# First-stage operand tiles placed for TensorE, all seven kinds at one distance from the weights, and a second copy of one kind's high parts

## The chip, the cores and the metric

One core of a Trainium2 chip runs the whole program as one launch. The metric is device time in microseconds, from start to end of one execution; the number quoted is the median of three runs, and one more execution was profiled. "us" is microseconds, "ns" nanoseconds.

## The reference

One layer of a hybrid decoder, 512 positions of width 2048, all in float32. With `h = RMSNorm(x)` it computes

```
proj = h @ w_in                      # 2048 x 5648: q, k, v | z, xBC, dt
x    = x + concat(attention, ssd_scan) @ w_out
u    = causal_conv3(RMSNorm(x) @ w_up)          # 2048 x 11264
x    = x + (silu(u_gate) * u_val) @ w_down      # 5632 x 2048
```

The products with `w_in`, `w_out`, `w_up` and `w_down` are nearly all of the arithmetic. The rest (8 heads of attention, the chunked scan of 16 heads, norms, convolutions) runs beside them.

## The kernel before

**Split products.** Every float32 operand of a large product is held as two tiles of the one-pass type: `hi`, a rounded copy that ScalarE makes, and `lo`, the remainder that VectorE subtracts. A product is three matmuls that add up in PSUM: hi by hi, hi by lo, lo by hi. Each matmul is preceded by a load of its own 128x128 weights (PEld in the profile), and that load runs while the matmul before it streams its moving operand.

**First stages** (`w_in`, then `w_out`). The weights come in chunks of 128x1024, three `raw` buffers deep, and `issue_split` (line 243) makes of each piece of up to 528 columns an `hi` and an `lo` tile, three buffers of each, in the pool `w`. The activations lie in `A0..A15` (high parts) and `B0..B15` (low parts), 512 columns each, allocated right behind that pool. There are two ways to use a piece:
- `fm_uses` (line 639) and `wide_use` (line 657): the piece is the stationary operand, and A or B moves with 512 columns.
- `tok_use` (line 672): A or B is the stationary operand, and the piece moves, with 256 columns (v), 264 (z and dt of the first group) or 512 (z of the second group).

The order of the work between the pieces is fixed when the program is built, by the costs in `Paced` and by `advance`, which lets generators of the attention and the scan issue their parts between pieces.

**Second stage** (`w_up`, then `w_down`). A two-by-two scheme with seven products in the place of eight is used: each of 68 groups (44 of up, with 8 blocks of the contraction; then three passes of 8 groups of down, with 7, 8 and 7 blocks) makes seven products P1 to P7. The weights of a product are a sum or difference of raw blocks, split into `hi2` and `lo2` (three and two buffers of 128x1024, lines 1034 to 1051). The moving operand is one of seven kinds (`KT1`, `KT3`, `K11`, `KT2`, `K21`, `K22`, `KT4`), a tile [128, 2, 8, 256] with high parts at index 0 and low parts at index 1. P3 is the product whose kind is `K22`. The order of the products is a list, `items` (line 997): P5 of a group, P3 of the group before, P1, P4 of the group before, P6, P2, P7. Lines 1285 to 1292 issue a product: for each of the n blocks one matmul with the kind's high part (L1288) and one with its low part (L1289), both by the weights `hi2`; then n with the high part by `lo2` (L1291). So a product is 24 or 21 matmuls of 256 columns. `step_slot` (line 1256) then issues, in the same order on every engine's queue, events, the `lo2` split of the item two ahead, more events, and the `hi2` split three ahead.

The kinds of up are made once: five at the end of the first stages, `K22` and `KT4` by `x_split` (line 1126) at slots 2, 4, 5 and 6. Each pass of down makes its seven kinds anew from scratch memory, `b_load` and `b_split` (line 1088), two halves per kind, at slots written out by hand around the last groups of the pass before.

**Addresses.** Where a tile starts follows from the order and sizes of allocation. Take the *distance* of a matmul as the start of its moving operand less the start of the weights that are loaded beside it (those of the next matmul), modulo 512 bytes; a block of weights is 512 bytes wide, a moving block of 256 columns 1024, so the distance stays the same within a product. Before the change:
- Second stage: 448 bytes for six kinds, 0 for `K22`. `KT4` lies behind `K22` in the same pool with a spare tile of 112 floats (448 bytes) between them (line 1129).
- First stages: `hi` and `lo` are 528 floats, 2112 bytes, so each buffer is shifted by 64 bytes against the one before it, and the distance changes with the buffer and from one matmul of a triple to the next: for a stationary piece 384, 192, 384 in the first buffers, 320, 128, 320 in the second, 256, 64, 256 in the third; for a moving piece of 256 or 512 columns 128, 320, 128, then 192, 384, 192, then 256, 448, 256.

Of the kernel before, what the change touches and what calls it, by code (L numbers as in the profile page):

```python
# [20 lines left out]
F32 = mybir.dt.float32  # L21
F32R = mybir.dt.float32r
BF = mybir.dt.bfloat16
AF = mybir.ActivationFunctionType
OP = mybir.AluOpType
# [8 lines left out]
NF = FF // 128  # L34
# [15 lines left out]
PASSES = [(0, 7), (7, 8), (15, 7)]  # L50
# [10 lines left out]
KT1, KT3, K11, KT2, K21, K22, KT4 = range(7)  # L61
# [126 lines left out]
def body(ctx, tc, xT, wi, wz, wo, wu, wd0, wd1, wd2, pp, pf, outT, dbg={}):  # L188
    nc = tc.nc
    clk = {"pe": 0.0, "act": 0.0, "dve": 0.0, "pool": 0.0, "last": ("pe", 0.0)}  # L190
    V, A_, T, G = (Paced(e, k, clk) for e, k in
                   ((nc.vector, "dve"), (nc.scalar, "act"), (nc.tensor, "pe"), (nc.gpsimd, "pool")))

    consts = ctx.enter_context(tc.tile_pool(name="consts", bufs=1))
    pstack = ExitStack()
    psum = pstack.enter_context(tc.tile_pool(name="psum", bufs=4, space=bass.MemoryType.PSUM))
    dram = ctx.enter_context(tc.tile_pool(name="scratch", bufs=1, space=bass.MemoryType.DRAM))
    ab, cw, work = ExitStack(), ExitStack(), ExitStack()
    wpool = ab.enter_context(tc.tile_pool(name="w", bufs=3))
    abp = ab.enter_context(tc.tile_pool(name="ab", bufs=1))  # L200
    cpool = cw.enter_context(tc.tile_pool(name="c", bufs=1, side="right"))
    wk = work.enter_context(tc.tile_pool(name="work", bufs=1, side="right"))
# [2 lines left out]
    def acc_tile():  # L205
        return psum.tile([128, 512], F32, name="acc", bufs=5)
# [3 lines left out]


    RW = 1024
    BEHIND = 2.5
    pieces = []

# [14 lines left out]
    def issue_dma(upto):  # L230
        while state["dma"] <= min(upto, len(raw_q) - 1):
            ci = state["dma"]
            src, width = raw_q[ci]
            r = wpool.tile([128, RW], F32, name="raw")
            if ci == 0:
                nc.sync.dma_start(r[:, :512], src[:, :512])
                nc.sync.dma_start(r[:, 512:width], src[:, 512:])
            else:
                nc.sync.dma_start(r[:, :width], src)
            raws[ci] = r  # L240
            state["dma"] += 1

    def issue_split(upto):
        while state["split"] <= min(upto, len(pieces) - 1):
            i = state["split"]
            ci, o, w, _ = pieces[i]
            issue_dma(ci)
            h = wpool.tile([128, 528], F32R, name="hi")
            l = wpool.tile([128, 528], F32R, name="lo")
            src = raws[ci][:, o:o + w]  # L250
            clk["last"] = ("pe", clk["pe"])
            A_.activation(h[:, :w], src, AF.Copy)
            V.tensor_tensor(l[:, :w], src, h[:, :w].bitcast(F32), op=OP.subtract)
            his[i] = (h, l)
            ready[i] = clk["dve"]
            state["split"] += 1
# [79 lines left out]
    def step(e):  # L336
        clk["last"] = ("pe", clk["pe"])
        old = clk["pe"], clk["act"], clk["dve"], clk["pool"]
        e[3] = 0
        try:  # L340
            say = next(e[0])
        except StopIteration:
            if e in gens:
                gens.remove(e)
            return
        if old != (clk["pe"], clk["act"], clk["dve"], clk["pool"]):
            e[1] = max(clk[k] for k in ("pe", "act", "dve", "pool") if k != "pool" or clk[k] != old[3]) + 0.3
        if e not in gens:
            e[2] = e[2] or say == "soon"
            gens.append(e)  # L350
        elif say == "soon":
            e[2] = True
        elif say == "later":
            e[2] = False

    def advance(force=False):

        for e in list(gens):
            e[3] += 1
            ready_ = clk["pe"] >= e[1]  # L360
            if force or (e[2] and (ready_ or e[3] > 1)) or \
                    (ready_ and max(clk["act"], clk["dve"]) < clk["pe"] + BEHIND):
                step(e)
# [308 lines left out]
    def tok_use(k0, nk, cols, box, done):  # L672

        def use(h, l):
            if k0 == 0:
                box["acc"] = [acc_tile() for _ in range(4)]
            edge = k0 == 0 or k0 + nk == NK
            order = [(kk, t) for t in range(4) for kk in range(nk)] if edge else \
                    [(kk, t) for kk in range(nk) for t in range(4)]
            for kk, t in order:  # L680
                k = k0 + kk
                ts_ = slice(t * 128, (t + 1) * 128)
                cc = slice(kk * cols, (kk + 1) * cols)
                o = box["acc"][t][:, :cols]
                T.matmul(o, A[k][:, ts_], h[:, cc], start=k == 0, stop=False)
                T.matmul(o, A[k][:, ts_], l[:, cc], start=False, stop=False)
                T.matmul(o, B[k][:, ts_], h[:, cc], start=False, stop=k == NK - 1)
                if k == NK - 1:
                    done(t, box["acc"][t])
        return use  # L690

    XR = lambda k: (A[k], B[k])
# [99 lines left out]
    for half in range(2):  # L792
        box = {}
# [68 lines left out]
    def cmb_tile(t):  # L862

        pool = p2["cmb"] if t < K22 else p2["cmbl"]
        return pool.tile([128, 2, 8, 256], F32R, name="cmb%d" % t)
# [62 lines left out]
    for i in range(4, NK):  # L928
        box = {}
# [39 lines left out]
    ve, se, pe, po, sy = nc.vector, nc.scalar, nc.tensor, nc.gpsimd, nc.sync  # L969
    lp = ctx.enter_context(tc.tile_pool(name="w2", bufs=1, reuse_waits="tile"))  # L970
# [8 lines left out]
    up_kinds = p2["kinds"]  # L979
    for i in range(NF):  # L980
        groups.append(dict(ph="up", i=i, n=8, kinds=up_kinds,
                           src={"11": wu[4 * i], "12": wu[4 * i + 1], "21": wu[4 * i + 2], "22": wu[4 * i + 3]}))
    for p, (f, n) in enumerate(PASSES):
        kinds = [None] * 7
        for m in range(NK // 2):
            w = (wd0, wd1, wd2)[p][m]
            groups.append(dict(ph="down", p=p, m=m, n=n, kinds=kinds,
                               src={"11": w[0], "12": w[1], "21": w[2], "22": w[3]}))
# [14 lines left out]
    cols = lambda gi: groups[gi]["n"] * 128  # L1003
# [52 lines left out]
    def at(slot, fn, *args, where=events):  # L1056
        where.setdefault(slot, []).append(lambda: fn(*args))
# [30 lines left out]
    def b_split(k):  # L1088
        p, t, h = b_list[k]
        ph = [g for g in groups if g["ph"] == "down" and g["p"] == p][0]["kinds"]  # L1090
        m = PASSES[p][1] - 4 if h else 4
        if h == 0:
            ph[t] = cmb_tile(t)
        ld = lds.pop(0)
        hi, lo = (ph[t][:, x, 4 * h:4 * h + m, :] for x in range(2))
        se.activation(hi, ld[:, :m, :], AF.Copy)
        ve.tensor_tensor(lo, ld[:, :m, :], hi.bitcast(F32), op=OP.subtract)  # L1097

    def down_pool():
        up_stack.close()  # L1100
        box["pool"] = ctx.enter_context(tc.tile_pool(name="down", bufs=1, side="right", reuse_waits="tile"))
        box["depth"] = 5

    for p in range(len(PASSES)):
# [10 lines left out]
        if p == 0:  # L1115
            at(base + 19, down_pool, where=after)


    x_ld = []

    def x_load(n):
        if n < 4:
            x_ld.append(side_tile(box["pool"], [4, 256], "ld", 3))
            sy.dma_start(x_ld[n], xd[:, 4 * (n % 2):4 * (n % 2) + 4, n // 2, :])

    def x_split(n):
        t, h = (K22, KT4)[n // 2], n % 2
        if n == 2:
            lp.tile([128, 112], F32, name="space")
        if h == 0:  # L1130
            up_kinds[t] = cmb_tile(t)
        o = up_kinds[t][:, :, 4 * h:4 * h + 4, :]
        se.activation(o[:, 0], x_ld[n], AF.Copy)
        ve.tensor_tensor(o[:, 1], x_ld[n], o[:, 0].bitcast(F32), op=OP.subtract)
        x_load(n + 3)

    for n, slot in enumerate((2, 4, 5, 6)):
        at(slot, x_split, n)
# [2 lines left out]
    box = {}  # L1141
# [114 lines left out]
    def step_slot(slot):  # L1256
        run(slot)
        if slot > -2:
            split_lo(slot + 2)
        run(slot, after)  # L1260
        split(slot + 3)
# [12 lines left out]
    for k, (gi, x) in enumerate(items):  # L1274
        g = groups[gi]
        if x == "P5":
            g["X"] = box["ps"].tile([128, 512], F32, name="x")
        if x == "P2":
            g["Y"] = box["ps"].tile([128, 512], F32, name="y")
        out = g["Y"][:, :256] if x == "P2" else g["X"][:, 256:] if x in ("P5", "P3") else g["X"][:, :256]  # L1280
        h, l = parts.pop(k)
        bk = g["kinds"][KIND[x]]
        n = g["n"]
        fresh = x in ("P5", "P2")
        for part in ((range(n - 1), range(n - 1, n)) if k < 2 else (range(n),)):
            for q in part:
                w = h[:, q * 128:(q + 1) * 128]
                pe.matmul(out, w, bk[:, 0, q, :], start=fresh and q == 0, stop=False, skip_group_check=True)  # L1288
                pe.matmul(out, w, bk[:, 1, q, :], start=False, stop=False, skip_group_check=True)  # L1289
            for q in part:  # L1290
                pe.matmul(out, l[:, q * 128:(q + 1) * 128], bk[:, 0, q, :], start=False, stop=q == n - 1,  # L1291
                          skip_group_check=True)
        if k == 0:
            start_up()
        (up_after if g["ph"] == "up" else down_after)(g, x)
        step_slot(k)
# [23 lines left out]
```

## Time and profile before

| | us |
|---|---|
| median of 3 runs (2103.43 to 2105.51) | 2104.23 |
| the profiled execution, its own time | 2103.83 |
| its span, first to last instruction | 2102.1 |
| PE busy in the span | 2061.9 |
| VectorE (DVE) busy | 1582.6 |
| ScalarE (ACT) busy | 988.3 |

The profile has a row for every instruction. A matmul's row gives some 0.28 us for 256 columns and 0.39 for 512, but matmuls overlap: what one costs is the time from its start to the start of the next, and a row that merges eight gives that best by its start and the start of the row behind it. PE is the matmul, PEld the load of weights that runs beside it.

### The profile page before, as it was taken

The numbers are of one execution on the slowest core, as the hardware profiler recorded it, in microseconds if no ns is written. First come the engines' busy times: TensorE is split into PE (matmuls) and PEld (weight loads), VectorE is DVE, ScalarE is ACT, GpSimd is POOL, SyncE is SP. The second block draws the span as 40 slices with busy tenths as digits, with TensorE's granted clock in tenths as the row PEclk, the third lists the DMA queues.
The fourth block names the chain that finished last, engine by engine and source line by source line (L and its number), as shares of the span: only waits on it lengthen the run. The fifth ranks groups of instructions, "written<-read, shape, count | busy, mean of one in ns | idle before, by whom it ended". The sixth has DMA issues, their size and how long they took to land.

```text
span 2102.1 us, 37694 instructions
## 1 busy us (share of the span) xinstructions
PE 2061.9 (98%) x15366; PEld 1938.7 (92%) x15366; DVE 1582.6 (75%) x2251; ACT 988.3 (47%) x1433; POOL 207.9 (10%) x107
## 2 busy tenths in 40 slices
PE   9999999999999998999999999999999899999999
PEld 7888887888888888999999999999999799899999
DVE  6545555345565548999999999999999977977976
ACT  5433435244444435555555554555555534534532
POOL 0020000000000001101110111111111111101110
PEclk9999999999999999999999999999999999999999
DMA  5232222332224445445444444444355667856753
GB/s 196 73 116 91 71 72 79 92 109 81 79 72 162 158 134 193 158 152 191 151 154 178 167 162 159 165 181 161 141 191 202 216 214 245 272 188 232 261 202 121
DMA packets 114397, 328.19 MB, mean 156 GB/s; under 512 B 10736, under 2 KB 35120, under 8 KB 111408
## 3 DMA queue, kind: packets, MB, share of 16 engines
q1 hardware_dynamic: 114224, 325.78, 45.0%
q8 instruction: 121, 1.98, 0.4%
q14 instruction: 52, 0.43, 0.1%
HBM read 283.77 MB, written 41.98 MB: 155 GB/s over the span
## 4 chain that ended last, share of the span: by engine, by line
PE 90%; DVE 6%; DMA 2%; issue 1%; ACT 1%; SPq 0%; DVEq 0%; POOL 0%; ACTq 0%; POOLq 0%
PE acc L183 30%; PE x L1288 16%; PE x L1289 16%; PE x L1291 16%; PE sm L183 4%; PE y L1288 3%; PE y L1289 3%; PE y L1291 3%; DVE lo L1050 1%; DVE cmb L1097 1%; DMA rawa<-wd 1%; DMA ld<-gd 0%; DVE lo L183 0%; DVE acc L1153 0%; DVE s L1024 0%
## 5 line engine op out<-in xcount | busy, mean ns | idle before, releaser
L1289 PE MATMUL x<-cmb,hi 128*128 128x256 f32 x3168 | 748.5, 278 | 13.2 <-DVE cmb L1097 11.5
L1288 PE MATMUL x<-cmb,hi 128*128 128x256 f32 x3168 | 749.1, 278 | 11.9 <-ACT cP L1168 5.4
L1289 PEld LDWEIGHTS x<-cmb,hi 128*128 128x128 f32 x3168 | 597.4, 189 | 16.1 <-DVE cmb L1097 14.3
L1288 PEld LDWEIGHTS x<-cmb,hi 128*128 128x128 f32 x3168 | 596.9, 188 | 14.4 <-issue 7.9
L1291 PE MATMUL x<-cmb,lo 128*128 128x256 f32 x3168 | 430.3, 278 | 2.2 <-DVE lo L1050 2.0
L1291 PEld LDWEIGHTS x<-cmb,lo 128*128 128x128 f32 x3168 | 393.4, 189 | 2.7 <-DVE lo L1050 2.7
L183 DVE TENSOR_TENSOR lo<-raw,hi 128x512 fp32r<-128x512 f32 (+1 forms) x240 | 164.4, 691 | 242.3 <-ACT hi L183 227.7
L1041 ACT ACTIVATE hi<-s 128x1024 fp32r<-128x1024 f32 (+1 forms) x201 | 200.8, 999 | 284.8 <-DVE s L1024 190.4
L1017 POOL TENSOR_TENSOR rawb<-rawa,rawb 128x1024 f32<-128x1024 f32 (+1 forms) x68 | 169.6, 2495 | 1298.3 <-DVE s L1024 1061.8
L183 PE MATMUL acc<-A,hi 128*128 128x512 f32 x704 | 281.5, 400 | 0.7 <-ACT hi L183 0.7
L183 PE MATMUL acc<-A,lo 128*128 128x512 f32 x704 | 277.9, 395 | 0.1
L183 PE MATMUL acc<-B,hi 128*128 128x512 f32 x704 | 276.9, 393 | 0.0
L183 ACT ACTIVATE hi<-raw 128x512 fp32r<-128x512 f32 (+1 forms) x240 | 149.6, 629 | 255.7 <-PE acc L183 222.5
L1050 DVE TENSOR_TENSOR lo<-s,hi 128x1024 fp32r<-128x1024 f32 (+1 forms) x201 | 238.4, 1186 | 18.8 <-issue 18.8
L1050 DVE TENSOR_TENSOR lo<-rawa,hi 128x1024 fp32r<-128x1024 f32 (+1 forms) x204 | 241.5, 1184 | 3.9 <-PE x L1291 3.9
L1041 ACT ACTIVATE hi<-rawa 128x1024 fp32r<-128x1024 f32 (+1 forms) x204 | 209.6, 1028 | 40.2 <-PE x L1289 40.0
L183 PEld LDWEIGHTS acc<-A,lo 128*128 128x128 f32 x704 | 132.2, 188 | 32.3 <-DVE lo L183 1.4
L183 PEld LDWEIGHTS acc<-A,hi 128*128 128x128 f32 x704 | 132.8, 189 | 29.0 <-ACT hi L183 1.3
L183 PEld LDWEIGHTS acc<-B,hi 128*128 128x128 f32 x704 | 132.5, 188 | 28.3
L1168 ACT ACTIVATE cP<-x 128x256 f32<-128x256 f32 x132 | 50.8, 384 | 211.2 <-PE x L1291 211.2
L183 PE MATMUL acc<-hi,A 128*128 128x256 f32 (+2 forms) x448 | 135.5, 302 | 0.7 <-DVE u L183 0.7
L183 PE MATMUL acc<-lo,A 128*128 128x256 f32 (+2 forms) x448 | 133.7, 298 | 0.0
(204 smaller groups left out, 2775.1 us busy)
## 6 DMA issues: line engine op xcount, KB each, us to landing
rawa<-wu SPq DMA_DIRECT2D x176, 512.0 KB, 3.3
raw<-wi SPq DMA_DIRECT2D x79, 512.0 KB, 3.6
rawa<-wd SPq DMA_DIRECT2D x64, 448.0 KB, 4.2
rawb<-wu SPq DMA_DIRECT2D x44, 512.0 KB, 4.3
gd<-gt SPq DMA_DIRECT2D x22, 1024.0 KB, 4.4
raw<-wo SPq DMA_DIRECT2D x32, 512.0 KB, 3.5
rawa<-wd SPq DMA_DIRECT2D x32, 512.0 KB, 4.4
ld<-gd SPq DMA_DIRECT2D x27, 512.0 KB, 6.3
```

The costliest lines, as they stand in the source:

```text
L183: return fn(out, *args, **kw)
L1017: po.tensor_tensor(r, raw[gi, "11"][:, :n], r, op=OP.subtract)
L1041: se.activation(h[:, :n], src[:, :n], AF.Copy)
L1050: ve.tensor_tensor(l[:, :n], src[:, :n], h[:, :n].bitcast(F32), op=OP.subtract)
L1097: ve.tensor_tensor(lo, ld[:, :m, :], hi.bitcast(F32), op=OP.subtract)
L1168: se.activation(g[x], X[:, 256:] if x == "P5" else X[:, :256], AF.Copy)
L1288: pe.matmul(out, w, bk[:, 0, q, :], start=fresh and q == 0, stop=False, skip_group_check=True)
L1289: pe.matmul(out, w, bk[:, 1, q, :], start=False, stop=False, skip_group_check=True)
L1291: pe.matmul(out, l[:, q * 128:(q + 1) * 128], bk[:, 0, q, :], start=False, stop=q == n - 1, skip_group_check=True)
```

## The change

The tiles `hi` and `lo` become 640 floats wide (2560 bytes, a whole multiple of 512), so that all their buffers, A and B have one remainder by 512. A use may ask for its piece to start 112 floats into the tile; `tok_use` asks for that where it moves fewer than 512 columns. So the distance becomes 0 for every 512-column matmul of these stages, 448 for those of 256, and 448 and 480 in turn for the blocks of 264.

In the second stage the spare tile of 448 bytes is put before `K22` instead of before `KT4`, so that all seven kinds have 448. Behind `KT4` come 64 spare bytes and a new tile `twin`, which thereby lies at distance 0; ScalarE copies the high parts of `K22` into it, once for up and once for each pass of down. P3 takes its high parts from `twin` in 14 groups: 1, 2, 4, 15 and 30 of up, and 1, 2 and 4 of each pass. There P3 is issued as n matmuls with the low parts (from `K22` itself, distance 448), n with `twin` by `hi2` and n with `twin` by `lo2` (both distance 0).

```diff
+    WT, BEHIND_256 = 640, 112
...
-            h = wpool.tile([128, 528], F32R, name="hi")
-            l = wpool.tile([128, 528], F32R, name="lo")
+            c = getattr(pieces[i][3], "at", 0)
+            h = wpool.tile([128, WT], F32R, name="hi")[:, c:c + w]
+            l = wpool.tile([128, WT], F32R, name="lo")[:, c:c + w]
...
+        use.at = BEHIND_256 if cols < 512 else 0      # in tok_use
...
+        if t == K22 and h:                            # in b_split
+            twin(ph, PASSES[p][1])
...
+    def twin(kinds, n):
+        box["twin"] = lp.tile([128, 8, 256], F32R, name="twin")
+        A_.activation(box["twin"][:, :n, :], kinds[K22][:, 0, :n, :].bitcast(F32), AF.Copy)
...
-        if n == 2:                                    # in x_split
-            lp.tile([128, 112], F32, name="space")
+        if n == 0:
+            space(lp, 448)
...
+        if n == 3:
+            space(lp, 64)
+            twin(up_kinds, 8)
...
+        if x == "P3" and (gi in (1, 2, 4, 15, 30) or gi >= NF and g["m"] in (1, 2, 4)):
+            tw = box["twin"]
+            for a, b, last in ((h, bk[:, 1], False), (h, tw, False), (l, tw, True)):
+                for q in range(n):
+                    pe.matmul(out, a[:, q * 128:(q + 1) * 128], b[:, q, :], start=False,
+                              stop=last and q == n - 1, skip_group_check=True)
```

`space(pool, n)` allocates n bytes per partition that nothing uses. No transfer is added, removed or moved, and no matmul is added or removed.

## Rows read from the trace of the kernel before

**Rows 1.** The page's first part (engine, busy us, share of the span, instructions), the row of granted clock from its second part, and the first line of its fourth part (the chain that ended last, by engine).
```profile
PE 2061.9 (98%) x15366; PEld 1938.7 (92%) x15366; DVE 1582.6 (75%) x2251; ACT 988.3 (47%) x1433; POOL 207.9 (10%) x107
PEclk9999999999999999999999999999999999999999
PE 90%; DVE 6%; DMA 2%; issue 1%; ACT 1%; SPq 0%; DVEq 0%; POOL 0%; ACTq 0%; POOLq 0%
```

**Rows 2.** Busy time by stretch: start and end in us, length, then busy us and instructions of PE, PEld, DVE, ACT and POOL, granted clock, DMA share and GB/s. The first row lies in the first stages, the second in up, the last at the turn from up to down.
```profile
200.00:400.00 200.00, 197.15 (x1076) 166.15 (x1076) 105.19 (x197) 86.77 (x164) 6.73 (x8) 1.00 0.26 80
1000.00:1200.00 200.00, 200.00 (x1753) 200.00 (x1752) 188.09 (x235) 103.56 (x134) 27.06 (x11) 1.00 0.45 163
1640.00:1720.00 80.00, 67.24 (x553) 64.30 (x552) 71.60 (x95) 39.09 (x46) 10.79 (x4) 1.00 0.70 239
```

**Rows 3.** PE in order of time in up, group 20 and 21 (start us, us, engine, line, operation, out<-in, count). From 1202.10 to 1204.96 it is a P3 (kind `K22`), from 1204.96 to 1207.70 a P1, from 1213.14 to 1215.86 a P2 (the one product whose output is named y).
```profile
1202.10 0.28 PE L1288 MATMUL x<-cmb,hi 128*128 128x256 f32 x1
...
1204.00 1.12 PE L1291 MATMUL x<-cmb,lo 128*128 128x256 f32 x8
1204.96 0.29 PE L1288 MATMUL x<-cmb,hi 128*128 128x256 f32 x1
...
1206.80 1.07 PE L1291 MATMUL x<-cmb,lo 128*128 128x256 f32 x8
1207.70 0.28 PE L1288 MATMUL x<-cmb,hi 128*128 128x256 f32 x1
...
1213.14 0.28 PE L1288 MATMUL y<-cmb,hi 128*128 128x256 f32 x1
...
1214.95 1.07 PE L1291 MATMUL y<-cmb,lo 128*128 128x256 f32 x8
1215.86 0.28 PE L1288 MATMUL x<-cmb,hi 128*128 128x256 f32 x1
```

**Rows 4.** The weight loads within one product (line, engine, operation, count, busy us, mean ns of one, idle before): of the P3 of rows 3 (1202.3 to 1204.7).
```profile
L1289 PEld LDWEIGHTS x<-cmb,hi 128*128 128x128 f32 x7 | 1.3, 190 | 0.0
L1288 PEld LDWEIGHTS x<-cmb,hi 128*128 128x128 f32 x7 | 1.3, 190 | 0.0
L1291 PEld LDWEIGHTS x<-cmb,lo 128*128 128x128 f32 x7 | 0.9, 192 | 0.0
```

**Rows 5.** The same within the product before that P3 (1199.4 to 1201.9), a P5.
```profile
L1289 PEld LDWEIGHTS x<-cmb,hi 128*128 128x128 f32 x8 | 1.5, 188 | 0.0
L1288 PEld LDWEIGHTS x<-cmb,hi 128*128 128x128 f32 x8 | 1.5, 188 | 0.0
L1291 PEld LDWEIGHTS x<-cmb,lo 128*128 128x128 f32 x8 | 1.0, 188 | 0.0
```

**Rows 6.** The groups of matmuls of the first stages, shapes apart (count, busy us, mean ns, idle before). The other two matmuls of each triple have the same count.
```profile
L183 PE MATMUL acc<-A,hi 128*128 128x512 f32 x704 | 281.5, 400 | 0.7 <-ACT hi L183 0.7
L183 PE MATMUL acc<-hi,A 128*128 128x256 f32 x256 | 73.5, 287 | 0.0
L183 PE MATMUL acc<-hi,A 128*128 128x264 f32 x128 | 36.8, 288 | 0.7 <-DVE u L183 0.7
L183 PE MATMUL acc<-hi,A 128*128 128x512 f32 x64 | 25.1, 392 | 0.0
```

**Rows 7.** Pieces of the chain that ended last (start us, us, what, count): a stretch of `w_out` with 512 moving columns of A and B, one of the second group's z with 512 moving columns of the pieces, and one of v with 256.
```profile
646.30 136.41 PE acc L183 x587
378.74 49.80 PE acc L183 x216
473.85 16.96 PE acc L183 x144
```

**Rows 8.** Busy time of the instructions that write or read the tiles acc, in a stretch of the 264-column blocks (columns as in rows 2, without POOL).
```profile
100.00:120.00 20.00, 20.00 (x166) 20.00 (x166) 0.86 (x4) 1.76 (x4) 1.00 0.41 118
```

**Rows 9.** PE in order of time at the start of up (columns as in rows 3): from 811.99 a P7 of group 0, kind at distance 448, after the waits of the first groups; up to 818.08 the end of a P5, then P3 of group 0 (distance 0), P1 of group 1 and, from 823.70 to 826.42, P4 of group 0.
```profile
811.99 0.28 PE L1288 MATMUL x<-cmb,hi 128*128 128x256 f32 x1
...
813.87 1.10 PE L1291 MATMUL x<-cmb,lo 128*128 128x256 f32 x8
814.82 0.60 PE L183 MATMUL y<-identf,rstd 128*128 128x128 f32 x4
...
817.14 1.11 PE L1291 MATMUL x<-cmb,lo 128*128 128x256 f32 x8
818.08 0.28 PE L1288 MATMUL x<-cmb,hi 128*128 128x256 f32 x1
...
823.70 0.28 PE L1288 MATMUL x<-cmb,hi 128*128 128x256 f32 x1
...
826.42 0.28 PE L1288 MATMUL x<-cmb,hi 128*128 128x256 f32 x1
```

**Rows 10.** ACT in order of time at the turn from up to down: the split of the second half of `K22` (L1096, 1670.67) and what is queued behind it.
```profile
1670.67 0.84 ACT L1096 ACTIVATE cmb<-ld 128x768 fp32r<-128x768 f32 x1 [2.15 <-DMA ld<-gd]
1671.42 0.80 ACT L1186 ACTIVATE tg<-ug,par 128x512 f32<-128x512 f32 x1
1672.97 1.05 ACT L1096 ACTIVATE cmb<-ld 128x1024 fp32r<-128x1024 f32 x1
```

**Rows 11.** DVE there, the work that waits for it.
```profile
1671.55 0.96 DVE L1097 TENSOR_TENSOR cmb<-ld,cmb 128x768 fp32r<-128x768 f32 x1 [0.61 <-ACT cmb L1096]
1672.42 0.74 DVE L1187 SCALAR_TENSOR_TENSOR tg<-ug,par,tg 128x512 f32<-128x512 f32 x1
```

More of the change, by code (lines that the diff above doesn't have):

```diff
@@ L192, in body @@
                    ((nc.vector, "dve"), (nc.scalar, "act"), (nc.tensor, "pe"), (nc.gpsimd, "pool")))
+    spaces = iter(range(100))
     consts = ctx.enter_context(tc.tile_pool(name="consts", bufs=1))
@@ L199, in body, with space @@
     wpool = ab.enter_context(tc.tile_pool(name="w", bufs=3))
+    def space(pool, n):
+        pool.tile([128, n // 4], F32, name="space%d" % next(spaces), bufs=1)
     abp = ab.enter_context(tc.tile_pool(name="ab", bufs=1))
@@ L247, in issue_split @@
             issue_dma(ci)
-            h = wpool.tile([128, 528], F32R, name="hi")
-            l = wpool.tile([128, 528], F32R, name="lo")
+            c = getattr(pieces[i][3], "at", 0)
+            h = wpool.tile([128, WT], F32R, name="hi")[:, c:c + w]
+            l = wpool.tile([128, WT], F32R, name="lo")[:, c:c + w]
             src = raws[ci][:, o:o + w]
             clk["last"] = ("pe", clk["pe"])
-            A_.activation(h[:, :w], src, AF.Copy)
-            V.tensor_tensor(l[:, :w], src, h[:, :w].bitcast(F32), op=OP.subtract)
+            A_.activation(h, src, AF.Copy)
+            V.tensor_tensor(l, src, h.bitcast(F32), op=OP.subtract)
             his[i] = (h, l)
@@ L1284, in body @@
         fresh = x in ("P5", "P2")
+        if x == "P3" and (gi in (1, 2, 4, 15, 30) or gi >= NF and g["m"] in (1, 2, 4)):
[4 more added lines that the diff above has]
+                              stop=last and q == n - 1, skip_group_check=True)
+            (up_after if g["ph"] == "up" else down_after)(g, x)
+            step_slot(k)
+            continue
         for part in ((range(n - 1), range(n - 1, n)) if k < 2 else (range(n),)):
```

## The prediction

> **What bounds the kernel now.** I read the engines' shares and the chain first. PE is busy for 98% of the span, nine tenths of the chain that ended last is PE, and the granted clock is full nearly throughout [rows 1]. By stretch: in the first stages PE is busy for 197 of 200 us while VectorE and ScalarE are at half or less; in up PE is busy without a gap, but VectorE stands at 188 of 200; at the turn from up to down PE drops to 67 of 80 us and VectorE is at 72 [rows 2]. So a faster matmul shortens the run almost everywhere, in up with only some 6% to go before VectorE sets the pace, and not at the turns.
>
> Then I read what one matmul costs, from start to start. A P2 in up takes 2.72 us for 24 matmuls, 113.3 ns each; P3, the one kind at distance 0, takes 2.86, and its last eight 0.96, 120 ns each [rows 3]. `KT4`, in the same pool, with the same shape and writer but 448 bytes off, is not slow: up runs in a steady 114.1 ns (1753 matmuls in 200 us) [rows 2], which is one product in seven at 119 and six at 113.3. Within P3 the weight loads take 190 to 192 ns against 188 elsewhere [rows 4, 5]. So the distance does it, and the load itself is late by part of it.
>
> In the first stages the distances change from matmul to matmul, and the cost lies between: 136.41 us for 587 matmuls of 512 columns are 232.4 ns, 49.80 for 216 are 230.6, 16.96 for 144 of 256 columns are 117.8 [rows 7]; 20 us for 166 in the 264-column blocks are 120.5 [rows 8]. Last, distance 448 has a second rhythm, the late phase: after the waits at the start of up a P7 at 448 ran 16 matmuls in 1.88 us, 117.5 ns [rows 9].
>
> **The change part by part.** The sum is made against the profiled execution, 2103.8 us, 0.4 below the median shown; I add that back at the end.
>
> *P3.* One P3 and the P1 behind it, whose first matmuls are slow as well, take 2.86 + 2.74 against twice 2.72: 0.16 us to win per group of 8 blocks, 0.14 with 7 [rows 3]. Of 68 groups 54 have no twin (39 of up and 5 of the pass with 8 blocks, 10 with 7): 44 x 0.16 + 10 x 0.14 = 8.4. In the 14 twin groups only the eight matmuls with the low parts move to 448, a third: 0.7. Together **9.1 us**.
>
> *What the old P3 also did.* The late phase at 448 costs 117.5 - 113.3 = 4.2 ns per matmul, 0.10 us per product. At the start of up it still holds in the P5 of group 1 (its last eight take 0.94 us, 117.5 ns each); then P3 passes at distance 0, and the P4 after the next product takes 2.72 us again [rows 9]. Now every kind is at 448, and the first product with distance 0 after a disturbance is the twin's P3 of group 1, seven products later: 0.7 us there, and as much at each turn if the waits leave PE in it. Between 0 and 2.8; I take **-1.0**, since only the start shows it plainly.
>
> *The twin's copies.* ScalarE copies 2048 elements four times (1792 in two of them). 1024 take 1.05 us [rows 10], so each is an estimated 1.9. In up ScalarE is half idle [rows 2], which hides it. At the first turn nothing does: the copy stands behind the second half of `K22` at 1671.5, ahead of the convolution (1671.42) and of the next split (1672.97) [rows 10], and VectorE takes the convolution's result at 1672.42, right after it is made [rows 11]; VectorE is the late engine there. Bounds: 0, and 4 x 1.9 = 7.6. I take **-1.5**, one turn's worth less a little, since the row shows only there a queue with no slack.
>
> *The turns.* PE waits for VectorE there [rows 2], so the six P3 of the groups on either side of three turns bring nothing: 6 x 0.15 = **-0.9**. Second stage: 9.1 - 1.0 - 1.5 - 0.9 = **5.7 us**. VectorE goes from 94% to some 95% of up, still under PE.
>
> *256 and 264 columns.* 3 x 256 = 768 matmuls [rows 6] go from 117.8 to a constant 448, where the second stage shows 113.3 or, in the late phase, 117.5. These blocks are cut up by other matmuls of the attention, so both will occur; the middle, 115.4, gives 768 x 2.4 = **1.8 us** (0.2 to 3.5). For 264 columns 113.3 scales to 116.8 against 120.5; with one block in two at 480, which no row shows, I take half of the 3.7: 384 x 1.85 = **0.7** (0 to 1.4).
>
> *512 columns.* This is the largest and least known term: 3 x 704 + 3 x 64 = 2304 matmuls [rows 6] go to a constant 0. No stretch shows 512 columns at constant 0. The nearest rows are the 256-column ones: twice the best is 226.7, twice the constant 0 is 240, and today's mixture is 232. For: of the 6.7 ns by which constant 0 is slower at 256 columns, up to 4 appear as a later weight load [rows 4, 5]; beside 512 columns the load, which is over after 188 ns of a 232 ns step, has time to spare, so that part would not count. That leaves some 2.7 on top of 226.7: 229.4, and 2304 x 2.6 = 6.0. Against: 0 was the worst value at 256. I take 229.0, **6.9 us**, with the ends 226.7 (+12.2) and 240 (-18.4).
>
> The wider tiles cost no time by themselves: ScalarE and VectorE write as many elements as before. No transfer is touched, and no product waits for a twin that is written shortly before it: the copy is made near the end of the splits, the first reader is P3 of group 1, at least one group of 19 us later.
>
> Sum: 5.7 + 1.8 + 0.7 + 6.9 = 15.1; 2103.8 - 15.1 = 2088.7, plus 0.4: **2089 us**.
>
> One rule speaks against all of this. The Trainium skill, page "SBUF — State Buffer", section "Who interferes with whom", gives TensorE two independent read ports, one for the moving operand and one for the weights, and says that "PE and ACT never wait on anyone"; the address of an operand plays no part in it. By that rule the sum would be nothing but the copies. The trace differs: 120 against 113.3 ns for two kinds that differ in their address alone.
>
> **The rivals.**
> - *512 columns stay as they are* (a constant 0 costs what the mixture costs, as at 256 columns: 120 against 117.8). Then the sum is 8.2 and the time 2096. For: 120 and 117.8 are close. Against: the load's slack.
> - *512 columns at their best*, 226.7: 2104.2 - 8.2 - 12.2 = 2084.
> - *Slower: 512 columns settle at 240*, twice the constant 0. The place is the first stages, the price 2304 x 8 = 18.4, less the 8.2: 2114. It decides from a mean above 232 + (8.2 + 4.2)/2.304 = 237.4 ns. For: the one constant 0 that the trace shows is the slowest rhythm there is. Against: at 256 columns the load fills the whole step.
> - *The late phase holds on.* With no P3 at 0 in groups 5 to 14, 16 to 29 and 31 to 43, a flip in up costs 0.7 us per group until the next twin. For: rows 9. Against: it followed long waits, and PE has none in up [rows 2]. One such stretch of 14 groups: 2089 + 10 = 2099.
> - *The distance is not the cause*, as that page's rule would have it: only the copies and the order of P3 remain, 1.5 us, 2106. The rows on `K22` and `KT4` speak against it.
>
> **How the numbers follow.** A measurement of this kernel can tell some 0.2%, 4.2 us, from no change. Forecast 0.42 (2085 to 2093), unchanged 512 columns 0.28 (2093 to 2099), their best 0.07, slower 0.10, late phase 0.07, no effect 0.06. The range 2078 to 2102 holds all but the slower case, the last one and the tails. Faster means below 2100: 0.42 + 0.27 + 0.07 + half of the late phase, 0.79; slower 0.12, same 0.09.
>
> **What would show it.** In the profile after: P3 without twin at 2.72 us and weight loads of 188 ns in it; P3 with twin with sixteen matmuls at 120; no product of up at 117.5 beyond group 1; the `w_out` stretch at about 229 ns per matmul and v at 115; ScalarE's four copies near 1.9 us and a convolution at the first turn later by that much. I am wrong if the `w_out` stretch lies above 232, or if up keeps 117.5 for whole groups.

## The result, and the profile after

The changed kernel takes **2088.75 us** (median of 4 runs, 2087.68 to 2091.87), against 2104.56 (4 runs, 2103.43 to 2105.51) for the kernel before on the same chip: a ratio of 0.9927, 95% interval 0.9911 to 0.9943. 2089.0 was forecast. The profiled execution has a span of 2086.9 us, 15.2 less than before.

The first two fences answer to [rows 1] and [rows 2]: shares of the engines, then busy time by stretch (the last window lies at the turn from up to down, which now comes some 15 us earlier).

```profile
PE 2048.4 (98%) x15366; PEld 1934.0 (93%) x15366; DVE 1581.2 (76%) x2251; ACT 994.9 (48%) x1437; POOL 208.1 (10%) x107
PE 90%; DVE 6%; issue 1%; DMA 1%; ACT 1%; SPq 0%; DVEq 0%; POOL 0%; ACTq 0%; POOLq 0%
```

```profile
200.00:400.00 200.00, 196.94 (x1084) 167.18 (x1083) 105.13 (x197) 86.76 (x163) 6.74 (x8) 1.00 0.27 80
1000.00:1200.00 200.00, 200.00 (x1766) 200.00 (x1765) 189.30 (x236) 106.81 (x138) 24.65 (x10) 1.00 0.48 166
1625.00:1705.00 80.00, 68.20 (x545) 65.11 (x545) 71.37 (x94) 40.88 (x47) 11.45 (x4) 0.98 0.70 238
```

The bound has not changed: the same 15366 matmuls, PE at 98%, and 13 more of them in the same 200 us of up (1766 for 1753, 113.3 ns each for 114.1). The turn is much as it was, PE waiting and VectorE at 71 of 80 us; the granted clock has 0.98 there for 1.00 before.

A P3 without a copy, in order of time (start, us, engine, line), answers to [rows 3]; its weight loads (count, busy us, mean ns) to [rows 4]:

```profile
1191.33 0.28 PE L1317 MATMUL x<-cmb,hi 128*128 128x256 f32 x1
...
1193.14 1.07 PE L1320 MATMUL x<-cmb,lo 128*128 128x256 f32 x8
1194.05 0.28 PE L1317 MATMUL x<-cmb,hi 128*128 128x256 f32 x1
```

```profile
L1318 PEld LDWEIGHTS x<-cmb,hi 128*128 128x128 f32 x8 | 1.5, 188 | 0.0
L1317 PEld LDWEIGHTS x<-cmb,hi 128*128 128x128 f32 x7 | 1.3, 188 | 0.0
L1320 PEld LDWEIGHTS x<-cmb,lo 128*128 128x128 f32 x8 | 1.0, 188 | 0.0
```

2.72 us in the place of 2.86, and loads of 188 ns in the place of 190 to 192. In the first stages, the pieces of the chain that answer to [rows 7], and the 264-column stretch of [rows 8]:

```profile
640.59 133.10 PE acc L183 x587
375.65 48.99 PE acc L183 x216
469.33 16.96 PE acc L183 x144
```

```profile
100.00:120.00 20.00, 20.00 (x167) 20.00 (x166) 0.84 (x4) 1.76 (x4) 1.00 0.41 118
```

512 columns at a constant 0 take 133.10 / 587 = 226.7 ns, as stationary pieces and as moving ones (48.99 / 216 = 226.8). This stretch of v took 16.96 us before and takes 16.96 now, and the 264-column stretch has one matmul more.

Over all matmuls, from start to start (ordinary steps only: under 300 ns for 512 columns, under 135 for the others; worked out from the trace):

| group | matmuls | before, ns | after, ns |
|---|---|---|---|
| 512 columns, piece stationary | 2112 | 231.74 | 227.55 |
| 512 columns, piece moving (z) | 192 | 230.49 | 226.67 |
| 256 columns, v | 768 | 117.93 | 116.14 |
| 264 columns | 384 | 121.67 | 121.22 |
| second stage | 11087 | 114.37 | 113.68 |

In us: 8.8 + 0.7 for 512 columns, 1.4 for v, 0.2 for 264. The second stage, with its waits, went from 1307.3 to 1300.9, 6.4 less. That is 17.5, of which 15.2 reached the span. Some 1.5 of the difference lies at the very start, where this execution ran its first matmuls of 512 columns at the pace of the lower level of the clock; the other 0.8 was not traced.

```profile
8.30 0.63 PE L183 MATMUL acc<-B,hi 128*128 128x512 f32 x1
...
10.42 0.40 PE L183 MATMUL acc<-A,hi 128*128 128x512 f32 x1
```

From 8.30 to 10.42 there are five steps of 424 ns; in the same five microseconds, 5 to 10, PE ran 12 matmuls here and 19 before. The trace has no record of the clock before 10.40 us, so the column of granted clock says nothing of these steps; that they are the lower level (1.2 GHz) is read from experiment 8, whose profiled execution alone among the nine below has them too, and where the granted clock is 0.50 from 9 to 10 us. Experiments 1, 3, 5 and 6 have the same first stages and start without them, so it seems to belong to the execution and not to the change.

**The start of up**, which answers to [rows 9]: the end of P5 of group 2, the P3 of group 1 through its copy (its first eight matmuls at 448, then eight and eight at 0), P1 of group 2 from 831.95, P4 of group 1 from 834.69.

```profile
828.73 0.52 PE L1320 MATMUL x<-cmb,lo 128*128 128x256 f32 x3
829.08 1.11 PE L1309 MATMUL x<-cmb,hi 128*128 128x256 f32 x8
830.02 1.12 PE L1309 MATMUL x<-twin,hi 128*128 128x256 f32 x8
830.98 1.12 PE L1309 MATMUL x<-twin,lo 128*128 128x256 f32 x8
831.95 0.28 PE L1317 MATMUL x<-cmb,hi 128*128 128x256 f32 x1
...
834.69 0.28 PE L1317 MATMUL x<-cmb,hi 128*128 128x256 f32 x1
...
837.41 0.28 PE L1317 MATMUL x<-cmb,hi 128*128 128x256 f32 x1
```

The first eight take 0.94 us, 117.5 ns: the late phase. The next sixteen, at distance 0, take 1.93, 120.6 ns. After them P1 takes 2.74 and P4 2.72: the late phase is over, and no product is in it again before the turn to down.

**At the first turn** the copy stands in ScalarE's queue ahead of the convolution (`tg`), and VectorE waits for that:

```profile
1655.82 1.70 ACT L183 ACTIVATE twin<-cmb 128x1792 fp32r<-128x1792 f32 x1
1657.42 0.80 ACT L1206 ACTIVATE tg<-ug,par 128x512 f32<-128x512 f32 x1
```

```profile
1658.26 0.75 DVE L1207 SCALAR_TENSOR_TENSOR tg<-ug,par,tg 128x512 f32<-128x512 f32 x1 [0.79 <-ACT tg L1206]
```

VectorE was idle for 0.79 us there, about half of the copy. The stretch from the P5 of group 43 to that of group 47 grew from 87.4 to 88.1 us. The clock was at its lower level in part of it (granted clock 0.50), which it was not at this turn before:

```profile
1665.90:1669.00 3.10, 3.10 (x17) 3.10 (x16) 3.07 (x7) 0.95 (x1) 0.00 (x0) 0.50 0.35 130
```

### The profile page after: what moved, and what is told of

Same layout as the page of the kernel before. It is cut to its first block, busy times and chain, and to the rows that moved or that the text cites. A ratio compares the mean times of both kernels' runs of the same rounds, so it can differ in the third digit from the quotient of the medians.

```text
span 2086.9 us, 37696 instructions
## 1 busy us (share of the span) xinstructions
PE 2048.4 (98%) x15366; PEld 1934.0 (93%) x15366; DVE 1581.2 (76%) x2251; ACT 994.9 (48%) x1437; POOL 208.1 (10%) x107
## 4 chain that ended last, share of the span: by engine, by line
PE 90%; DVE 6%; issue 1%; DMA 1%; ACT 1%; SPq 0%; DVEq 0%; POOL 0%; ACTq 0%; POOLq 0%
PE acc L183 30%; PE x L1320 15%; PE x L1317 15%; PE x L1318 15%; PE sm L183 4%; PE y L1317 3%; PE y L1320 3%; PE y L1318 3%; PE x L1309 2%; DVE lo L1060 2%; DVE cmb L1107 1%; DVE acc L1173 0%; DMA ld<-gd 0%; DVE s L1034 0%; DVE lo L183 0%
## 5 line engine op out<-in xcount | busy, mean ns | idle before, releaser
L1317 PE MATMUL x<-cmb,hi 128*128 128x256 f32 x3062 | 720.4, 278 | 12.4 <-ACT cP L1188 5.4
L1318 PE MATMUL x<-cmb,hi 128*128 128x256 f32 x3062 | 720.4, 278 | 11.6 <-DVE cmb L1107 11.6
L1317 PEld LDWEIGHTS x<-cmb,hi 128*128 128x128 f32 x3062 | 577.3, 189 | 14.9 <-issue 8.4
L1318 PEld LDWEIGHTS x<-cmb,hi 128*128 128x128 f32 x3062 | 577.4, 189 | 14.4 <-DVE cmb L1107 14.2
L1320 PE MATMUL x<-cmb,lo 128*128 128x256 f32 x3062 | 414.3, 277 | 1.0 <-DVE lo L1060 0.9
L1320 PEld LDWEIGHTS x<-cmb,lo 128*128 128x128 f32 x3062 | 379.0, 189 | 1.8 <-DVE lo L1060 1.8
L183 PE MATMUL acc<-hi,B 128*128 128x256 f32 (+2 forms) x448 | 132.7, 296 | 0.0
```

Source lines behind the costliest of these rows:

```text
L183: return fn(out, *args, **kw)
```

## The experiments

The theory to be tested: the pace of a matmul follows its distance; 512 columns gain by sitting at 0, the kinds by sitting at 448, and the copy is there to end the late phase. The rivals: the gain is in one half alone; the copies are a cost without a use; the order of P3's matmuls in the 14 groups does it, not the copy's address.

**1. The first stages' half alone** (`K22` stays at 0, no copies).

```
         if t == K22 and h:
-            twin(ph, PASSES[p][1])
...
-        if n == 0:
+        if n == 2:
             space(lp, 448)
...
-            space(lp, 64)
-            twin(up_kinds, 8)
...
-        if x == "P3" and (gi in (1, 2, 4, 15, 30) or gi >= NF and g["m"] in (1, 2, 4)):
+        if False:
```

> The first-stage half of the change alone; the second stage as before (K22 at distance 0, no twin). Theory A, the steps of the prediction: the two halves add up, so this one is worth the 8.9 us by which the first stages ended earlier in the changed kernel: 2104.5 - 8.9 = 2095.6, w_out at 226.7 ns per 512-column matmul, P3 still 2.86 us. Rival B: part of the gain of the first stages is really the second stage's (other start of up, other clock): then under 6 us, above 2098.

2094.12 us (4 runs, 2093.24 to 2094.64), ratio 0.995 (0.9935 to 0.9965): 10.7 us less than before. 512 columns take 227.57 ns, v 116.18, P3 is as it was, and the second stage sums to 1307.3 us, the same as before.

**2. The second stage's half alone.**

```
-    WT, BEHIND_256 = 640, 112
+    WT, BEHIND_256 = 528, 0
```

> The second-stage half alone (all kinds at 448, twin in 14 groups); the first stages with tiles of 528 floats as before. Theory A: worth what is left, 15.5 - 8.9 = 6.6 us: 2098, P3 without twin at 2.72 us, w_out at 232 ns per matmul. Rival B: the halves do not add up: below 2096 or above 2100.

2098.8 us (8 runs, 2097.16 to 2100.8), ratio 0.9974 (0.9963 to 0.9985): 6.0 us less (2104.8 to 2098.8). Stationary pieces of 512 columns take 231.77 ns as before, the second stage sums to 1300.9 us as with the whole change. 10.7 + 6.0 = 16.7 against 15.8 for both: within the intervals the halves add up, and neither is for nothing.

**3. Everything aligned, but no copy**: P3 runs at 448 in all groups.

```
         if t == K22 and h:
-            twin(ph, PASSES[p][1])
...
-            space(lp, 64)
-            twin(up_kinds, 8)
...
-        if x == "P3" and (gi in (1, 2, 4, 15, 30) or gi >= NF and g["m"] in (1, 2, 4)):
+        if False:
```

> The whole change without the twin: no copies, P3 in all 68 groups as the other products, at 448. Theory A: only matmuls at another distance, or a long wait, end the late phase; it begins in P2 of group 0 as in the changed kernel and holds through up, 43 groups x 7 products x 0.10 us = 30 us, until the waits at the turn to down: about 2088.7 + 28 = 2117. Rival B: the late phase ends by itself within a few groups and the twin is not needed: 2088.7 - 2 = 2087. Rival C: it ends by chance somewhere in up: between the two.

2116.99 us median of 10 runs, 9 of them from 2115.34 to 2120.71 and one at 2088.70; ratio 1.0043 (1.0015 to 1.0072). Up by stretch (columns as above):

```profile
1000.00:1200.00 200.00, 200.00 (x1701) 200.00 (x1700) 183.31 (x229) 101.78 (x131) 26.25 (x11) 1.00 0.45 160
```

1701 matmuls in 200 us, 117.6 ns each, where the changed kernel has 1766. The late phase begins in group 0 as it does there, and then holds through every product until the turn, over 800 us on. The second stage sums to 1330.2 us, 29.3 more. So without the copies the second stage's half is a loss: the copies carry it. By its time the run at 2088.70 lacks the late phase in up, so it does not hold in every execution.

**4. A sweep of distances**, one run: every kind at another distance, and in the first stages another distance for each accumulation (`sweep` counts the pieces, 16 floats are 64 bytes); no copies, as in 3.

```
+            use.at = 16 * (sweep["fm"] // 2 % 8)
...
-        use.at = BEHIND_256 if cols < 512 else 0
+        use.at = 16 * (k0 // 2) if cols == 512 else 16 * (6, 5, 4, 2)[sweep["v"] // 8] if cols == 256 else 104 - 8 * (sweep["z"] // 8)
...
         for t in (KT1, KT3, K11, KT2, K21):
+            space(p2["cmb"], 64)
...
-            space(lp, 448)
+            space(lp, 64)
...
+            if n == 2:
+                space(lp, 384)
```

> One look at many distances: the seven products of the second stage at different ones (P5 192, P7 256, P1 320, P6 384, P2 and P4 448, P3 64; no twin), the 512-column accumulations at 0, 448, 384, 320, 256, 192, 128, 64 in turn, z of the second group at 0 to 448 in steps of 64, the four blocks of v at 384, 320, 256, 128. Theory A: the value of a constant distance counts; at 512 columns 0 gives 226.7 ns and others lie up to 240; at 256 columns 448 gives 113.3 and others up to 120. Rival B: constancy is what helps at 512 columns, and every constant distance gives 226.7 within 1 ns. Rival C: 448 is best at 512 columns too and 0 only as good by chance.

2127.36 us. In `w_out` the pieces pass through the distances 448, 384, 320, 256, 192, 128, 64 and 0, 48 matmuls each. The first matmul of each block in order of time (the last row begins the next 448):

```profile
663.38 0.39 PE L183 MATMUL acc<-A,lo 128*128 128x512 f32 x1
...
674.57 0.39 PE L183 MATMUL acc<-A,lo 128*128 128x512 f32 x1
...
685.73 0.40 PE L183 MATMUL acc<-A,lo 128*128 128x512 f32 x1
...
696.73 0.39 PE L183 MATMUL acc<-A,lo 128*128 128x512 f32 x1
...
707.63 0.39 PE L183 MATMUL acc<-A,lo 128*128 128x512 f32 x1
...
718.83 0.39 PE L183 MATMUL acc<-A,lo 128*128 128x512 f32 x1
...
729.98 0.40 PE L183 MATMUL acc<-A,lo 128*128 128x512 f32 x1
...
740.98 0.39 PE L183 MATMUL acc<-A,lo 128*128 128x512 f32 x1
...
751.88 0.39 PE L183 MATMUL acc<-A,lo 128*128 128x512 f32 x1
```

Differences over 48: 233.1 ns at 448, 232.5 at 384, 229.2 at 320, 227.1 at 256, 233.3 at 192, 232.3 at 128, 229.2 at 64, 227.1 at 0. The series repeats after 256 bytes, and 0 is its best place. So the value of a constant distance counts (theory A, though nothing came near its 240), and constancy alone is not what helps (rival B). The kernel before had three buffers with 384, 192, 384, then 320, 128, 320, then 256, 64, 256; the mean of these nine by the sweep is 230.3, of the 231.7 that it took.

In `w_out` the weights are what is moved. In z of the second group it is the moving pieces, at 0, 64, 128, 192 and on to 448, with A and B as weights, 24 matmuls each. The first matmul of the first five blocks:

```profile
379.73 0.39 PE L183 MATMUL acc<-hi,A 128*128 128x512 f32 x1
...
385.18 0.40 PE L183 MATMUL acc<-hi,A 128*128 128x512 f32 x1
...
390.69 0.40 PE L183 MATMUL acc<-hi,A 128*128 128x512 f32 x1
...
396.27 0.40 PE L183 MATMUL acc<-hi,A 128*128 128x512 f32 x1
...
401.88 0.39 PE L183 MATMUL acc<-hi,A 128*128 128x512 f32 x1
```

Differences over 24: 227.1 ns at 0, 229.6 at 64, 232.5 at 128, 233.8 at 192, and the next four blocks repeat this. Moving the other operand gives the same pace at the same distance, so it is the offset between the two that counts, and not where either lies by itself.

In the second stage (P2 at 448 from 1200.19, P7 at 256, P5 at 192, P3 at 64 from 1208.62):

```profile
1200.19 0.28 PE L1322 MATMUL y<-cmb,hi 128*128 128x256 f32 x1
...
1203.02 0.28 PE L1322 MATMUL x<-cmb,hi 128*128 128x256 f32 x1
...
1205.89 0.29 PE L1322 MATMUL x<-cmb,hi 128*128 128x256 f32 x1
...
1208.62 0.28 PE L1322 MATMUL x<-cmb,hi 128*128 128x256 f32 x1
```

P2 at 448, behind the P6 at 384, takes 2.83 us, 117.9 ns, throughout up; P7 at 256 takes 2.87, where the P3 at 0 took 2.86 [rows 3]; P5 at 192, behind P7, takes 2.73 to 2.74, in all groups of up from the second on. P4, at 448 too, but behind P1 at 320, is at 113.6 in most groups. So a kind at 448 or 192 has two paces, and which it takes depends on what ran before it. That is not the distance of the product before alone: in down, in groups 46 to 51 and 61 to 67, which have 7 blocks, the same P2 behind the same P6 is quick; group 48:

```profile
1755.39 0.28 PE L1322 MATMUL y<-cmb,hi 128*128 128x256 f32 x1
...
1757.78 0.28 PE L1322 MATMUL x<-cmb,hi 128*128 128x256 f32 x1
```

2.39 us for 21 matmuls, 113.8 ns; in groups 53 to 59 of the pass with 8 blocks, between those, P2 is at 117.8 again.

**5. All kinds at 192**, no copies.

```
             p2["kinds"][t] = cmb_tile(t)
+        space(p2["cmb"], 256)
...
-            space(lp, 448)
+            space(lp, 192)
...
-            twin(up_kinds, 8)
...
+        if False:
```

> First stages as in the changed kernel, all seven kinds at a distance of 192 bytes instead of 448, no copies and no P3 through a copy. Theory A: the late phase is a property of the distance 448 (a product there takes 113 or 118 ns by what ran before it), and at 192 a product takes 113 whatever ran before, as P5 did at 192 in the sweep, in every group. Then the second stage's ordinary steps fall from a mean of 113.68 ns to 113.3, 11,087 x 0.38 = 4.2 us, and the copies' price goes too: 2084.5 us (2083 to 2086), with no product at 117 or more outside the waits. Rival B: P5 alone was quick at 192 because nothing late ran before it; with all kinds at 192 some start of the stage sets a late phase too, and without copies nothing ends it: 2110 to 2120 us, as without copies at 448. Rival C: the other kinds at 192 are at 120 or so as at 256: above 2120 us.

2121.15 us (5 runs, 2116.3 to 2122.53), ratio 1.0074 (1.0061 to 1.0087). Up:

```profile
1000.00:1200.00 200.00, 200.00 (x1701) 200.00 (x1700) 183.32 (x229) 101.73 (x131) 25.87 (x11) 1.00 0.44 159
```

My theory A fell: 192 is no better than 448, and in up the two are the same to the matmul. That fits the period of 256 bytes of the sweep, which I had not drawn on: 448 is 192 + 256. P5 was quick in the sweep, presumably because a product at 256 ran just before it. The profiled execution was also late through the second pass of down (groups 52 to 60), which the one of experiment 3 was not: the second stage sums to 1333.3 us here and to 1330.2 there.

**6. The copy itself moved to 448**, all else as in the changed kernel.

```
-            space(lp, 64)
             twin(up_kinds, 8)
```

> The changed kernel with the copy itself moved from a distance of 0 to one of 448 bytes; the copies, the 14 groups and the order of the matmuls in their P3 stay. Theory A: it is the distance of the copy that ends the late phase (its matmuls at 120 ns are out of step with the 118 of the phase), so that at 448 nothing ends it: 2117 us as without copies, with P3 of the 14 groups at 118 like the others. Rival B: it is the order of P3's matmuls in these groups (all of one term, then the next) that ends it: 2087 to 2089 us, the 14 P3s at 113 after their first matmuls.

10 runs fall in two groups: 7 from 2116.4 to 2122.67 and 3 from 2086.54 to 2091.84. Median 2117.25; the ratio's interval, 0.9955 to 1.003, mixes both groups and says little. The profiled execution is of the long kind:

```profile
1000.00:1200.00 200.00, 200.00 (x1701) 200.00 (x1700) 183.31 (x229) 101.80 (x132) 26.68 (x11) 1.00 0.45 160
```

With the same copies and the same order of P3's matmuls the late phase holds through up. So it is the address that ends it: the 16 matmuls at 0. Since some runs are short without it, the count is the evidence: with the copy at 0 none of 17 runs was long (the changed kernel, experiments 2 and 8); with no matmul of P3 at 0, here and in 3, 5 and 7, 32 of 37 were.

**7. As 5, and v's pieces at 192 too** (the 264-column ones at 192 and 224).

```
-    WT, BEHIND_256 = 640, 112
+    WT, BEHIND_256 = 640, 48
```

> As the kernel with all seven kinds at 192 bytes, and the first stages' 256-column pieces at 192 as well instead of 448 (the 264-column ones at 192 and 224). Theory A: these pieces too take 116.1 ns at 448 because they are partly in the late phase, and 113.3 at 192: 768 x 2.8 = 2.1 us less than with the kinds alone, 2082.4 us. Rival B: at the first stages the 256-column pieces are held by something else (the weights' own place), and stay at 116: the same time as with the kinds alone, within 0.5 us.

2117.81 us median of 12 runs, 11 from 2114.64 to 2127.59 and one at 2093.93; ratio 1.005 (1.003 to 1.0069). v takes 116.08 ns at 192, 116.14 at 448, with the same spread (a quarter of the steps at 113 or less, over half at 117 or more): again the same place modulo 256. So v stays at 116, as rival B had it, and theory A's 113.3 fell. The runs are 3.3 us shorter than those of experiment 5, but not by v: the second stage sums to 1328.6 us for 1333.3.

**8. The copy used in 4 groups, not 14.**

```
-        if x == "P3" and (gi in (1, 2, 4, 15, 30) or gi >= NF and g["m"] in (1, 2, 4)):
+        if x == "P3" and (gi == 1 or gi >= NF and g["m"] == 1):
```

> The changed kernel with P3 through the copy in 4 groups only (group 1 of the up stage and the second of each pass of down) instead of 14. Theory A: the late phase begins only where a stage starts or turns, and one P3 at a distance of 0 ends it for good; the other ten P3s only cost 16 matmuls x 6.7 ns = 0.11 us each: 2088.75 - 1.1 = 2087.7 us in every run. Rival B: something inside a stage sets the late phase again (a short wait, a stretch at the lower clock), and the ten are what ends it: some of the runs are then 5 to 25 us longer than the changed kernel.

2089.51 us (5 runs, 2087.38 to 2092.22), ratio 0.9928 (0.9914 to 0.9941): not to be told from the changed kernel. Up:

```profile
1000.00:1200.00 200.00, 200.00 (x1768) 200.00 (x1767) 189.48 (x236) 106.93 (x139) 24.62 (x10) 1.00 0.47 168
```

The second stage sums to 1299.9 us, 1.0 less than in the changed kernel, as ten P3s fewer should give (1.1). None of the 5 runs was longer for want of the ten, so in these runs one P3 at 0 behind each start or turn was enough.

**9. A finer sweep**, no copies: P5 at 96, P7 at 128, P1 at 160, P6 at 192, P2 at 224, P3 at 32, P4 at 96. One run.

```
-        for t in (KT1, KT3, K11, KT2, K21):
+        for t, n in ((KT1, 0), (KT3, 16), (K11, 32), (KT2, 16), (K21, 16)):
+            if n:
+                space(p2["cmb"], n)
...
+        space(p2["cmb"], 208)
...
-            space(lp, 448)
+            space(lp, 32)
...
+            if n == 2:
+                space(lp, 64)
```

> No copies; the kinds at distances that are odd multiples of 32 bytes and two that are not: P3 at 32, P4 at 96, the other five at 96, 128, 160, 192 and 224. One look, in which each kind's pace is read by itself. Theory A: the pace follows the distance modulo 256 without a step between the multiples of 64, so 224 and 160 lie between their neighbours, the kind at 192 takes 113 or 118 by what ran before it, and no distance is under 113.3. Rival B: 224 or 160 takes 113 in every group, with no late phase; then a kernel with all kinds there needs no copy. Time in all about 2115 to 2130 us by A.

2130.26 us. The expectation names the distances as a set; the tiles start at multiples of 32 bytes, so it was these seven. First matmuls, one product a row, of P1 of group 20 (1187.80), P4 of 19, then P6, P2 and P7 of 20 and P5 of 21 (1201.91):

```profile
1187.80 0.28 PE L1319 MATMUL x<-cmb,hi 128*128 128x256 f32 x1
...
1190.62 0.28 PE L1319 MATMUL x<-cmb,hi 128*128 128x256 f32 x1
...
1193.50 0.28 PE L1319 MATMUL x<-cmb,hi 128*128 128x256 f32 x1
...
1196.23 0.28 PE L1319 MATMUL y<-cmb,hi 128*128 128x256 f32 x1
...
1199.06 0.28 PE L1319 MATMUL x<-cmb,hi 128*128 128x256 f32 x1
...
1201.91 0.28 PE L1319 MATMUL x<-cmb,hi 128*128 128x256 f32 x1
```

P1 at 160 takes 2.82 us (117.5 ns), P4 at 96 2.88 (120), P6 at 192, behind it, 2.73 (113.8), P2 at 224 2.83 (117.9), P7 at 128 2.85 (118.8); P5 at 96 and P3 at 32, from the trace's steps, 119.7 and 116.6 ns. Only 192 comes near 113.3. Theory A holds, and there is no place among these that is quick and has no late phase.

## Why the prediction was right

**P3** (+9.1 foretold): right. A P3 takes 2.72 us, its loads 188 ns, and up runs at 113.3 ns. Experiment 2 has the second stage net at 6.4 in its sum and 6.0 in the runs, 5.7 foretold.

**The late phase** (-1.0): right in mechanism, and the step that mattered most. It began in P2 of group 0, held through ten products, P5 of group 2 included (the last before the P3 of group 1, and one more than "beyond group 1" allowed), and ended in the copy's P3 of group 1. From the P5 of group 0 to that of group 2 the time grew by 0.56 us (44.29 to 44.85), for 0.7 foretold. What I got wrong is its rank: "the late phase holds on" had a chance of 0.07 and one stretch of 10 us, and I priced the copies as a cost. Experiments 3 and 6 show that it can hold by itself for all of up, in most runs, and that it then costs 28 us. "It followed long waits, and PE has none in up" was a reason against its *starting* there; in experiment 3 it *stayed* without one. That no stretch came back in the changed kernel fits: each start and turn has a P3 at 0 behind it. [Rows 9] had shown this in small.

**The copies** (-1.5): they take 1.70 to 1.93 us (1.9 estimated), and at the first turn 0.79 us of it reached VectorE. The stretch of that turn lost 0.7 in all, less than I had set down. How much of it is the copy stays open: in the same stretch four products (P6, P2 and P7 of group 45, P5 of 46) were in the late phase, 0.4 by their number, and the granted clock was 0.50 for 3.1 us, in which P6 of group 45 took 3.16 us for 2.38 before; the P5 of 46, with its wait, then took 3.58 for 4.82. No run measures the price of all four copies by itself.

**512 columns** (+6.9): the mis-sized term. I took 229.0 ns; it is 226.7, which I had as the best end. "The load has time to spare, so that part would not count" holds, and the remaining 2.7 ns, which I left on top, do not count either. Measured 9.5 us at the steps, less the slow first matmuls of that execution. So an undisturbed stretch runs as the case "512 columns at their best" had it, but that case's 12.2 us did not come: over all of them the mean went from 231.6 only to 227.5 ns, since they did not all stand at 232 before and do not all reach 226.7 after. That the time came out 0.25 us from the forecast is in part luck: 2.6 more than foretold here and 0.7 more in the second stage stand against 0.9 less for v and 264 columns, 1.5 lost at the start of this execution and 0.8 not traced. In experiment 1, with v and 264 columns, the half gave 10.7 us where the sum had 9.4. The slower rival, 512 columns at 240 because the only constant 0 in the trace is the slowest pace, fell.

**256 and 264 columns** (+1.8, +0.7): v got 1.4; the stretch of [rows 7] stayed at 117.8 and others fell to 113, the two paces of 448 which I had expected to mix. 264 columns gained nearly nothing (121.67 to 121.22 ns), where I had scaled the best of 256.

**The distance is not the cause**: fell. Within experiment 4 the blocks of `w_out` differ in nothing but the address of the piece, and 512 columns move between 227.1 and 233.3 ns. The Trainium skill, page "SBUF — State Buffer", section "Who interferes with whom", has PE wait for no one at its two ports, and names no address. The trace disagrees in so far as the offset between the two operands sets PE's pace: by 2.7% at 512 columns and 5.9% at 256 (120 for 113.3).

**Open**: what inside the chip has the period of 256 bytes; what sets the late phase off at the start, and what before a product at 192 or 448 decides its pace (experiment 4 has one P2 both ways behind the same P6); and why 5 of the 37 runs of experiments 3, 5, 6 and 7 came out at 2086.5 to 2093.9. By their time they lack the late phase in up, but no profile was taken of one.

## What to carry to other kernels

Where PE is back to back, group its matmuls by the offset between the moving operand and the next weights, and compare the pace from start to start within each group: one that is 2 to 6% off, as here, may be had back by a spare tile or a wider one. Sweep the offset for each shape by itself, since 0 was the best place for 512 columns and the worst for 256. And before removing a slow step, ask what state it resets: here the slow P3 was also what ended the late phase, and 16 matmuls in its old place, once behind each start or turn, were worth 28 us.

## What was not expected of the hardware

- The pace depends on the distance modulo **256** bytes: at 512 columns 227.1, 229.2, 232.4, 233.2 ns at 0, 64, 128, 192 and the same again above; at 256 columns 120 at 0, 116.6 at 32, 117.8 at 64, 119.8 at 96, 118.8 at 128, 117.5 at 160, 113.3 or 117.8 at 192, 118.1 at 224 (each behind the kinds of its own run, so the small steps may be the neighbours'). Whole accumulations of v at 384, 320, 256 and 128 in experiment 4 bear three of these out: 118.8, 117.8, 119.9 and 118.7.
- At 192 (and 448) the pace has **two values that hold by themselves**. In up a product at 0 or 256 left the quick one behind and one at 384 the late one, but in most of the 7-block groups of down the same P6 at 384 left the quick one. The late one lasted over 800 us without a cause that the profile shows.
- The slow first steps of 424 ns are about what 512 columns take at 1.2 GHz (512 / 1.2 = 426.7), with nothing on top; at 2.4 GHz the best step is 226.7, against 213.3 for the columns alone. What the distance changes comes on top of that best.
